# The gate projected and applied token-major in an RWKV-7 mixer layer

## The chip, the cores and the metric
The kernel runs on one core of a Trainium2 chip. The metric is the device time of one execution in microseconds (us). The engines are TensorE (PE), VectorE (DVE), ScalarE (ACT), GpSimd (POOL) and SyncE (SP), which issues most of the transfers.

## The reference
One RWKV-7 time-mixing layer: 2048 tokens, width 1024, 16 heads of 64, all fp32. Cut to what matters:

```python
x_r, x_w, x_k, x_v, x_a, x_g = (h + dx * mu[i] for i in range(6))   # h: normed x
r, k, v = x_r @ W_r, x_k @ W_k, x_v @ W_v
g = silu(x_g @ W_g)
w_lo, a_lo = tanh(x_w @ w_dn), x_a @ a_dn        # low rank: decay and a
def step(S, inp):                                # per head, S is 64 x 64
    sa = einsum('vk,k->v', S, -kk_t)
    S = S * w_t[None, :] + sa[:, None] * (kk_t * a_t)[None, :] + v_t[:, None] * k_t[None, :]
    return S, einsum('vk,k->v', S, r_t)
y = (y - mean) * rsqrt(var + eps)                # per head
y = y * gn_w + gn_b
y = y + sum(r * k * r_k) * v
out = x + (y * g) @ W_out
```

## The kernel before, in words
The tokens are cut into 8 blocks of 256 (`TB`) and 64 chunks of 32 (`L`), the heads into 8 pairs. An fp32 matmul is done as three passes over high and low parts (`passes`, `proj` at L545: high by high, low by high, high by low), 8 column tiles `ct` of the contraction each. The work stands in three stages.

**Stage A** (to about 480 us) loops over the blocks. It norms x into `h`, makes the token-shift mixes of each projection (`mixa` for V, `mixb` for the gate, one buffer each, high and low parts `mixah`, `mixal` and so on), the low-rank products (`lps`, L607), stores the mixes of K and R in DRAM, and then projects. V is token-major: a tile `vps` has 128 tokens by 512 columns, the mix is stationary and 512 columns of W_v move; ACT copies it out (`vo`, L640), DVE subtracts the mean (`vc`, L51), both go to DRAM. The gate is channel-major: a tile `gps` has 128 of W_g's columns by 256 tokens, W_g is stationary and the mix moves, eight tiles a block. `gate` (L195 to L200) applies twice silu: ACT a tanh (`go`), DVE one operation (`go`), and the tile goes to `g_d[b]`, laid out [channel, column tile, token]. The framework's own scheduler orders this stage. In the last block W_r's loads follow.

**Stage B** (to about 1163 us) projects K and R, makes the chunks' operands and inverts their triangular parts; from here on the order is written by hand (`manual_schedule`), each engine in the order in which the program emits. Its end runs the first chunks' recurrence beside the last block.

**The recurrence** (about 1163 to 1656 us). `chunk` issues for each chunk two waves, each of them on PE the state part (`ybank`, L257), the state's update (`dp`, L282), the output part (`ybank`, L293) and `ubank` (L269), with ACT's copies behind them: `misc` L262, `x` L286, `y` L301, `x` L273. Between these, `fill` puts output-projection matmuls (`ops`, L465), by counts `F`. Elementwise work is popped from a queue by `background(BG)`: every step has a price in microseconds and a call spends 1.6 of them; a step of (None, None) ends a call.

The elementwise work is `tail(t)`, t from 0 to 15, one for every four chunks (128 tokens): squares on ACT, variances on DVE, three Newton steps for the reciprocal root on POOL (`rst`, L388), then in four parts of 128x256 the norm (`y<-y,rst` L51, `y<-y,aux` L415) and the bonus (`y<-y,v` L419), all on DVE. Then the two halves k of the tokens are transposed on PE (`yt`, L429, four 128x128 transposes each) into a PSUM bank of a pool `tps` that has one buffer. DVE adds gn_b to it (shift, in PSUM), multiplies it by the gate (gating, `gt<-yt,gt`), ACT takes the high part (`oh`, L444), DVE the low part (`ol`), and 48 output matmuls are queued for `fill`. Their results are added to x (`xr`, L48) and stored. The gate is loaded for the shift's turn from `g_d[b]` in 256-byte pieces, two transfers a tail. Behind the last chunk a loop runs `background(2)` and `fill(6)` until nothing is left.

Of the kernel before, what the change touches and what calls it, by code (L numbers as in the profile page):

```python
# [8 lines left out]
F32 = mybir.dt.float32  # L9
# [9 lines left out]
P = 128  # L19
D = 1024  # L20
# [15 lines left out]
PARAMS = ("norm", "mu_r", "mu_w", "mu_k", "mu_v", "mu_a", "mu_g", "w0", "a0", "k_k", "k_a", "r_k", "gn_b")  # L36
# [3 lines left out]
def rwkv7_kernel(ctx, tc, a, T):  # L40
# [43 lines left out]
    g_d = [dram.tile([P, NCT, TB], F32, name=f"g_d{b}") for b in range(NB)]  # L84
# [4 lines left out]
    # W_out's rows in the place of two blocks' mixes, once those are used  # L89
# [9 lines left out]
    def rsqrt(pool, out, x, shape, nm):  # L99
        # x in SBUF, positive and normal; out may not alias x  # L100
# [23 lines left out]
    def load_w(src, nm, stage, eng=lambda i: None):  # L124
        # steps that load a weight's rows, the row blocks in turn, and the access to its parts
# [24 lines left out]
    def load_wc(src, nm, stage):  # L150
        # the same by column blocks
# [25 lines left out]
    def load_mix(k, mix, b, pool=False, n=NCT // 2):  # L177
        # a projection's mix of the rows, 0: k, 1: r; the steps that split it
# [26 lines left out]
    # of half h: partitions of the K|V and of the B|U parts; columns of the A and of the R part  # L205
# [36 lines left out]
    def decay(ch):  # L242
        # diagonal blocks beside the token-major [K|B]: the chunk's decay of the state
# [59 lines left out]
    def chunk(ch, state, fill):  # L303
        # the recurrence's step, the second wave's end of the chunk before within it
# [28 lines left out]
    def fill(n):  # L333
        # n of the output projection's matmuls between the recurrence's small ones
# [9 lines left out]
    def tail(t):  # L344
        # norm, bonus, gate and output of chunks 4t to 4t + 3, in steps
# [74 lines left out]

        def transpose(k):
# [14 lines left out]
        four = lambda z: z.rearrange("p (h j) t -> p h j t", h=2)  # L436
# [54 lines left out]
    def inversion(g, z, tmp):  # L491
        # z: strict parts, rows (h, chunk, pair); their unit triangular inverses go into M
# [16 lines left out]
    with ExitStack() as p0:  # L509
# [37 lines left out]
        with ExitStack() as pa:  # L547
# [25 lines left out]
            # low rank weights of a token's own and of the token before's normed row  # L573
# [9 lines left out]
            def split_up():  # L583
                # the up projections' weights in high and low parts, stacked to contract at once
                for q in range(2):
                    ups = stage(f"ups{q}")
                    nc.sync.dma_start(ups, a["up"][:, 512 * q : 512 * q + 512])
                    parts = [sp.tile([P, 512], F32R, name=f"up{x}{q}", tag="vo") for x in "hl"]
# [7 lines left out]
            for b in range(NB):  # L596
# [36 lines left out]
                for n in range(2):  # L633
                    for q in range(2):
# [4 lines left out]
                        vo = sp.tile([P, 8, N], F32, name=f"vo{b}{q}{n}", tag="vo")  # L639
# [5 lines left out]
                        vc = sp.tile([P, 8, N], F32, name=f"vc{b}{q}{n}", tag="vo")  # L645
# [8 lines left out]
                for i in range(NCT):  # L654
                    ps = pps.tile([P, TB], F32, name=f"gps{b}{i}", tag="vg")
                    sl = slice(i * P, (i + 1) * P)
                    proj(ps, lambda c: wg[0](c, sl), lambda c: wg[1](c, sl), lambda c: mgh[:, c], lambda c: mgl[:, c])
                    gate(b, i, ps, sp)

        with ExitStack() as pb:  # L660
# [63 lines left out]
            def tokenmajor(c, bank):  # L724
                # [P = (j, i, h; 32), TB] sums to token-major [P, 2, (h, i, j)]
# [47 lines left out]
            def split_lo(b, raw):  # L773
                # high parts twice, beside the low ones: the up projections contract both parts of their weights at once
# [69 lines left out]
            def r_proj(b, p, ps):  # L844
                # the projection's matmuls in two halves
# [466 lines left out]
```

## Time and profile before

| | |
|---|---|
| runs | 1656.64, 1653.35, 1651.27 us |
| median | 1653.35 us |
| profiled execution | span 1656.3 us (of the runs, the one of 1656.64 us is nearest to it), granted clock 0.980 in the mean |
| PE, DVE, ACT, POOL busy | 94%, 71%, 56%, 35% of the span |
| DMA | 269.15 MB, 163 GB/s |

The span runs from the first to the last instruction. A busy PE is modelled, since matmuls overlap: the time that a matmul occupies PE is read from the distance of starts, not from its duration. The number behind x is how many instructions a row holds, and a bracket with an arrow tells how long the engine was idle ahead of the row and what ended that.

### The profile page before, as it was taken

The numbers are of one execution on the slowest core, as the hardware profiler recorded it, in microseconds if no ns is written. First come the engines' busy times: TensorE is split into PE (matmuls) and PEld (weight loads), VectorE is DVE, ScalarE is ACT, GpSimd is POOL, SyncE is SP. The second block draws the span as 40 slices with busy tenths as digits, with TensorE's granted clock in tenths as the row PEclk, the third lists the DMA queues.
The fourth block names the chain that finished last, engine by engine and source line by source line (L and its number), as shares of the span: only waits on it lengthen the run. The fifth ranks groups of instructions, "written<-read, shape, count | busy, mean of one in ns | idle before, by whom it ended". The sixth has DMA issues, their size and how long they took to land.

```text
span 1656.3 us, 46156 instructions
## 1 busy us (share of the span) xinstructions
PE 1549.2 (94%) x17776; PEld 1311.4 (79%) x17776; DVE 1179.6 (71%) x2592; ACT 932.4 (56%) x2378; POOL 573.1 (35%) x911
## 2 busy tenths in 40 slices
PE   3799999999999999989898989899999999999998
PEld 2589889998798887878787878787677777777776
DVE  7976776667656679897988888857646755765454
ACT  5653332233356455445445454588888778877771
POOL 4500000000002334333334343554556555565541
PEclk9899999999999999999999999999999999999999
DMA  5773433334563565656565657787877677667652
GB/s 183 223 259 125 141 124 106 128 125 155 156 215 111 131 136 134 130 152 139 149 151 144 146 145 150 186 223 222 208 202 197 179 189 201 175 167 206 176 126 86
DMA packets 445740, 269.15 MB, mean 163 GB/s; under 512 B 302768, under 2 KB 386096, under 8 KB 445520
## 3 DMA queue, kind: packets, MB, share of 16 engines
q1 hardware_dynamic: 444176, 261.67, 58.9%
q10 hardware_dynamic: 1344, 4.52, 0.9%
q8 instruction: 141, 2.31, 0.6%
q14 instruction: 79, 0.65, 0.1%
HBM read 158.74 MB, written 111.54 MB: 163 GB/s over the span
## 4 chain that ended last, share of the span: by engine, by line
PE 54%; DVE 20%; issue 6%; DMA 6%; ACT 5%; POOL 3%; SPq 0%; DVEq 0%; POOLq 0%; ACTq 0%
PE ops L465 11%; PE gps L545 10%; PE vps L545 5%; PE kps L545 4%; PE ybank L257 4%; PE rps L851 4%; PE ybank L293 3%; DVE th L809 3%; PE dp L282 3%; PE ubank L269 3%; DVE z L51 2%; DVE tm L51 2%; PE mps L887 2%; DVE bk L51 1%; PE lps L607 1%
## 5 line engine op out<-in xcount | busy, mean ns | idle before, releaser
L545 PE MATMUL gps<-mixbh,wgh 128*128 128x256 f32 x512 | 146.9, 287 | 5.0 <-ACT vo L640 5.0
L247 POOL TENSOR_TENSOR dk<-consts,misc 64x512 f32<-64x512 f32 x128 | 144.3, 1127 | 9.3
L545 PE MATMUL gps<-mixbl,wgh 128*128 128x256 f32 x512 | 146.7, 286 | 0.0
L545 PE MATMUL gps<-mixbh,wgl 128*128 128x256 f32 x512 | 146.7, 286 | 0.0
L545 PE MATMUL kps<-mixbl,wkh 128*128 128x256 f32 x448 | 130.7, 292 | 14.8 <-DVE mixbl L186 14.8
L851 PE MATMUL rps<-mixah,wrh 128*128 128x256 f32 x448 | 132.8, 296 | 2.1 <-ACT sq L60 2.1
L545 PE MATMUL kps<-mixbh,wkh 128*128 128x256 f32 x448 | 134.2, 300 | 0.2 <-DVE u L48 0.2
L545 PE MATMUL kps<-mixbh,wkl 128*128 128x256 f32 x448 | 129.8, 290 | 0.0
L851 PE MATMUL rps<-mixal,wrh 128*128 128x256 f32 x448 | 127.2, 284 | 0.0
L851 PE MATMUL rps<-mixah,wrl 128*128 128x256 f32 x448 | 127.1, 284 | 0.0
L60 ACT ACTIVATE th<-wa,dprm 128x256 f32<-128x256 f32 x64 | 30.4, 475 | 169.4 <-PE wa L803 93.9
L841 POOL TENSOR_TENSOR ra<-th,e 128x256 f32<-128x256 f32 x56 | 47.8, 854 | 211.6 <-DVE th L48 207.6
L97 POOL TENSOR_TENSOR upl<-ups,uph 128x512 fp32r<-128x512 f32 x2 | 2.6, 1287 | 336.3 <-DMA up_d<-uph 333.0
L222 POOL MEMSET x<- 32x512 f32 x128 | 66.4, 519 | 145.4 <-PE ybank L293 137.3
L545 PE MATMUL vps<-wvh,mixah 128*128 128x512 f32 x256 | 106.3, 415 | 5.8 <-ACT mixah L96 4.5
L262 ACT COPY misc<-ybank 32x256 f32<-32x256 f32 x220 | 79.9, 363 | 55.7 <-PE ybank L257 52.0
L465 PE MATMUL ops<-woh,oh 128*128 128x512 f32 x256 | 109.5, 428 | 1.6 <-ACT oh L444 1.6
L465 PE MATMUL ops<-woh,ol 128*128 128x512 f32 x256 | 110.4, 431 | 0.0
L465 PE MATMUL ops<-wol,oh 128*128 128x512 f32 x256 | 107.2, 419 | 0.0
L545 PEld LDWEIGHTS gps<-mixbh,wgh 128*128 128x128 f32 x512 | 99.9, 195 | 5.4 <-ACT vo L640 5.4
L545 PE MATMUL vps<-wvl,mixah 128*128 128x512 f32 x256 | 103.5, 404 | 0.0
L545 PEld LDWEIGHTS kps<-mixbl,wkh 128*128 128x128 f32 x448 | 89.1, 199 | 16.0 <-DVE mixbl L186 16.0
(326 smaller groups left out, 4909.4 us busy)
## 6 DMA issues: line engine op xcount, KB each, us to landing
stat<-sm_d SPq DMA_DIRECT2D x64, 512.0 KB, 5.0
dk<-bt_d SPq DMA_DIRECT2D x128, 128.0 KB, 4.6
sm_d<-ra SPq DMA_DIRECT2D x112, 128.0 KB, 3.2
sm_d<-mo SPq DMA_DIRECT2D x112, 128.0 KB, 2.7
bt_d<-bo SPq DMA_DIRECT2D x56, 256.0 KB, 3.3
up<-up_d SPq DMA_DIRECT2D x66, 128.0 KB, 2.7
xn<-x SPq DMA_DIRECT2D x32, 256.0 KB, 4.4
mkr_d<-mok SPq DMA_DIRECT2D x64, 128.0 KB, 1.9
```

The source lines that it names most:

```text
L51: return nc.vector.tensor_tensor(out=out, in0=in0, in1=in1, op=op)
L222: nc.gpsimd.memset(x[bu(h), h], 0.0)
L247: nc.gpsimd.tensor_tensor(out=dk[ch % len(dk)][H, h], in0=ident[H, None, H].broadcast_to([64, NP, N]), in1=pls[g][H, c, :, None].broadcast ...
L257: nc.tensor.matmul(y[half(h), p], st[:, h, 4 * w + p], x[:, h, 4 * w + p], start=(p == 0), stop=(p == 3), tile_position=(0, 64 * h))
L262: nc.scalar.copy(gs[bu(h)], y[kv(h)])
L269: nc.tensor.matmul(bank[2][rb, p], st[rb, h, 4 * w + p, ca], gs[rb, p], start=True, stop=True, tile_position=(rb.start, rb.start))
L282: nc.tensor.matmul(dp[half(1 - h), p], d[:, h, 4 * w + p], x[:, h, 4 * w + p], start=True, stop=True, tile_position=(0, 64 * (1 - h)))
L293: nc.tensor.matmul(bank[w][rb, ch % 2, p], st[rb, h, 4 * w + p, cr], x[rb, h, 4 * w + p], start=False, stop=(p == 3), skip_group_check=Tru ...
L465: nc.tensor.matmul(ps, l[:, ct], r(ct, ns), start=(ct == 0 and k == 0), stop=(ct == NCT - 1 and k == 2))
L545: nc.tensor.matmul(ps, x, y, start=first, stop=last)
L809: nc.vector.tensor_tensor_scan(th, rmask.rearrange("p c l -> p (c l)"), th, 0.0, mul, add)
L851: nc.tensor.matmul(ps, x, y, start=first, stop=last)
```

## The change
The gate's projection takes V's form: 128 tokens by 512 columns, the mix stationary, 512 columns of W_g moving, four tiles a block, and `gate` evacuates tiles of 128x512 (`go` shares the three buffers of `vo` and `vc`). `g_d` becomes one [token, channel] table with rows of 2 KB for a transfer. The tail loads it ahead of the norm, in four transfers, and applies gn_b and the gate to the token-major y in SBUF: a new step `gating(c)` of two DVE operations of 128x256 behind each part's bonus. gn_b moves from the column parameters to `aux`, beside gn_w. Behind the transposes stands only the split: `high` (ACT, `oh` from PSUM) and `rest` (DVE, `ol` from PSUM and `oh`). Shift and the old gating fall away. `rest(0)` is emitted behind the second transposes and their `high`.

```diff
-    def gate(b, i, ps, pool, tag="go", bufs=2):
-        go = pool.tile([P, TB], F32, name=f"go{b}_{i}", tag=tag, bufs=bufs)
+    def gate(rows, ns, ps, pool, nm):
+        go = pool.tile([P, 512], F32, name=f"go{nm}", tag="vo", bufs=3)
         act(go, ps, AF.Tanh, scale=0.5)
         stt(go, go, 1.0, ps, add, mul)
-        nc.sync.dma_start(g_d[b][:, i], go)
+        nc.sync.dma_start(g_d[rows, ns], go)
...
+        def gating(c):
+            x, i = y[part(c)], part(c)[2]
+            tt(x, x, al["gb"][:, i], add)
+            tt(x, x, st["g", c // 2][:, i], mul)
...
         def load_gate(k):
-            st["g", k] = al["gt"](f"gt{t}{k}")
-            nc.sync.dma_start(st["g", k], g_d[b][:, :, q * P + 64 * k : q * P + 64 * k + 64])
+            st["g", k] = g = al["gt"](f"gt{t}{k}")
+            r0 = t * P + 64 * k
+            for h in range(2):
+                nc.sync.dma_start(g[half(h)], g_d[r0 : r0 + 64, 512 * h : 512 * h + 512].rearrange("t (p n) -> t p n", n=N))
...
-        def shift(k):
-            gb = prm[:, PI["gn_b"]].rearrange("p (h j) -> p h j", h=2)
-            tt(turn(k), turn(k), gb[..., None].broadcast_to([P, 2, 4, 64]), add)
-
-        def gating(k):
-            tt(four(st["g", k]), turn(k), four(st["g", k]), mul)
-            nc.scalar.copy(st["oh"][:, :, 64 * k : 64 * k + 64], st["g", k])
+        def high(k):
+            nc.scalar.copy(four(st["oh"], k), turn(k))
 
         def rest(k):
-            tok = slice(64 * k, 64 * k + 64)
-            tt(st["ol"][:, :, tok], st["g", k], st["oh"][:, :, tok].bitcast(F32), sub)
+            tt(four(st["ol"], k), turn(k), four(st["oh"], k).bitcast(F32), sub)
...
+        out.append((0.0, lambda: (load_gate(0), load_gate(1))))
         for c in range(4):
             out.append((0.7, lambda c=c: norm(c)))
             out.append((0.4, lambda c=c: bonus(c)))
+            out.append((0.7, lambda c=c: gating(c)))
         cut = len(out)
-        out.append((0.0, lambda: (load_gate(0), load_gate(1))))
         for k in range(2):
-            out.extend([(None, None), (0, lambda k=k: transpose(k)), (None, None)])
+            out.extend([(None, None), (0, lambda k=k: transpose(k)), (None, None), (0, lambda k=k: high(k))])
             if k == 1:
                 out.append((0.7, lambda: rest(0)))
-            out.append((0.7, lambda k=k: shift(k)))
-            out.append((0.7, lambda k=k: gating(k)))
         out.append((0.7, lambda: rest(1)))
...
-                for i in range(NCT):
-                    ps = pps.tile([P, TB], F32, name=f"gps{b}{i}", tag="vg")
-                    sl = slice(i * P, (i + 1) * P)
-                    proj(ps, lambda c: wg[0](c, sl), lambda c: wg[1](c, sl), lambda c: mgh[:, c], lambda c: mgl[:, c])
-                    gate(b, i, ps, sp)
+                for n in range(2):
+                    for q in range(2):
+                        rows, ns = slice((2 * b + q) * P, (2 * b + q + 1) * P), slice(n * 512, (n + 1) * 512)
+                        ps = pps.tile([P, 512], F32, name=f"gps{b}{q}{n}", tag="vg")
+                        proj(ps, lambda c: mgh[:, c, q * P : (q + 1) * P], lambda c: mgl[:, c, q * P : (q + 1) * P],
+                             lambda c: wg[0](c, ns), lambda c: wg[1](c, ns))
+                        gate(rows, ns, ps, sp, f"{b}{q}{n}")
```

How the change moves instructions shows at three places. In the rows yt120 is the bank's tile of tail 12, half 0, and yt121 that of half 1; y12 is the tail's normed y, ops110 an output tile of tail 11; the numbers behind an underscore are buffers.

First PE's queue between the two transposes of tail 12, in the changed kernel:

```order
L434 MATMUL yt120_21093<-consts_60,y12_19756 128x128 x4
L282 MATMUL dp_14785<-x1_12923,dk2_12920 64x64 x8
L466 MATMUL ops110_21072<-wol1_13498,oh11_20641 128x512
L466 MATMUL ops110_21072<-woh1_13497,ol11_20642 128x512
L293 MATMUL ybank1_14783<-x1_12923,stat2_12916 32x64 x8
L269 MATMUL ubank_14784<-misc_12911,stat3_12917 32x64 x8
L466 MATMUL ops110_21072<-woh2_13689,oh11_20641 128x512
L466 MATMUL ops110_21072<-wol2_13690,oh11_20641 128x512
L466 MATMUL ops110_21072<-woh2_13689,ol11_20642 128x512
L466 MATMUL ops110_21072<-woh3_13870,oh11_20641 128x512
L257 MATMUL ybank1_14783<-x2_12924,stat3_12917 64x64 x8
L434 MATMUL yt121_21154<-consts_60,y12_19756 128x128 x4
```

One wave, with six output matmuls, stands between the two sets, as it did before; what the second set waits for has changed from DVE's gating to DVE's `ol` of the first half.

Second ACT's queue at the same place: before (first fence) and in the changed kernel (second).

```order
L273 COPY x1_13858<-ubank_15713 32x256 x2
L262 COPY misc_13846<-ybank1_15712 32x256 x2
L444 CAST oh12_21613<-gt120_21562 128x8x64
L286 COPY x2_13859<-dp_15714 64x256 x2
L301 COPY y13_21264<-ybank0_15711 32x256 x2
```

```order
L301 COPY y14_20799<-ybank1_14783 32x256 x2
L273 COPY x2_12924<-ubank_14784 32x256 x2
L446 CAST oh12_21091<-yt120_21093 128x8x64
L262 COPY misc_12911<-ybank1_14783 32x256 x2
L286 COPY x0_12922<-dp_14785 64x256 x2
```

The cast of the first half's high part stood behind `misc` and read SBUF; now it stands between the wave's last copy `x` and the next wave's `misc`, and reads the bank.

Third DVE's queue at the same tail: before (first fence) and in the changed kernel (second).

```order
L419 TENSOR_TENSOR y12_20740<-y12_20740,v12_1_21301 128x256
L48 SCALAR_TENSOR_TENSOR xr1010_21427<-ops101_21426,xr1010_21427 128x256
L48 SCALAR_TENSOR_TENSOR xr1011_21429<-ops101_21426,xr1011_21429 128x256
L51 TENSOR_TENSOR yt120_21615<-yt120_21615,prm_62 128x2x4x64
L51 TENSOR_TENSOR gt120_21562<-yt120_21615,gt120_21562 128x512
L51 TENSOR_TENSOR ol12_21614<-gt120_21562,oh12_21613 128x8x64
L51 TENSOR_TENSOR yt121_21678<-yt121_21678,prm_62 128x2x4x64
L51 TENSOR_TENSOR gt121_21564<-yt121_21678,gt121_21564 128x512
L51 TENSOR_TENSOR ol12_21614<-gt121_21564,oh12_21613 128x8x64
```

```order
L51 TENSOR_TENSOR y12_19756<-y12_19756,rst12_20744 128x256
L415 TENSOR_TENSOR y12_19756<-y12_19756,aux_12912 128x256
L419 TENSOR_TENSOR y12_19756<-y12_19756,v12_1_20748 128x256
L48 SCALAR_TENSOR_TENSOR xr1010_20836<-ops101_20835,xr1010_20836 128x256
L48 SCALAR_TENSOR_TENSOR xr1011_20838<-ops101_20835,xr1011_20838 128x256
L51 TENSOR_TENSOR y12_19756<-y12_19756,aux_12912 128x256
L51 TENSOR_TENSOR y12_19756<-y12_19756,gt121_20898 128x256
L51 TENSOR_TENSOR ol12_21092<-yt120_21093,oh12_21091 128x8x64
L51 TENSOR_TENSOR ol12_21092<-yt121_21154,oh12_21091 128x8x64
```

Each part of y has five operations instead of three, and the two `ol` now stand together behind all twenty, with nothing between them.

## Rows read from the trace of the kernel before

**Rows 1.** The page: busy time, share of the span and instructions of each engine

```profile
PE 1549.2 (94%) x17776; PEld 1311.4 (79%) x17776; DVE 1179.6 (71%) x2592; ACT 932.4 (56%) x2378; POOL 573.1 (35%) x911
```

**Rows 2.** Stretches: us; busy (x) PE, PEld, DVE, ACT, POOL; PEclk, DMA share, GB/s

```profile
240.00:280.00 40.00, 40.00 (x280) 37.51 (x280) 25.45 (x67) 10.78 (x27) 0.00 (x0) 1.00 0.36 123
...
1400.00:1500.00 100.00, 99.35 (x1763) 74.75 (x1763) 70.66 (x142) 80.50 (x218) 57.93 (x96) 1.00 0.68 180
```

**Rows 3.** The chain of waits in stage A: start us, us, what

```profile
145.93 17.27 PE gps L545 x144
...
163.79 8.20 PE vps L545 x36
```

**Rows 4.** PE's timeline in the recurrence: start us, us, instruction, count

```profile
1388.22 0.69 PE L257 MATMUL ybank<-x,stat 128*64 128x64 f32 x16
...
1391.64 0.69 PE L257 MATMUL ybank<-x,stat 128*64 128x64 f32 x16
1392.25 0.66 PE L429 MATMUL yt<-consts,y 128*128 128x128 f32 x4
...
1395.79 0.69 PE L257 MATMUL ybank<-x,stat 128*64 128x64 f32 x16
```

**Rows 5.** ACT's timeline: the same waves, and a cast near the end

```profile
1391.30 0.76 ACT L273 COPY x<-ubank 32x256 f32<-32x256 f32 x2
1392.42 0.75 ACT L262 COPY misc<-ybank 32x256 f32<-32x256 f32 x2 [0.37 <-PE ybank L257]
...
1620.56 0.62 ACT L444 CAST oh<-gt 128x512 fp32r<-128x512 f32 x1
```

**Rows 6.** Stage A's evacuations by form: duration in ns, min/median/max

```profile
L48 DVE SCALAR_TENSOR_TENSOR go<-go,gps x64: 409/421/423, 88.2 to 480.2; 128x256 f32<-128x256 f32 x64
...
L640 ACT COPY vo<-vps x32: 574/587/590, 73.4 to 463.1; 128x512 f32<-128x512 f32 x32
...
L51 DVE TENSOR_TENSOR vc<-vo,mn x32: 677/691/694, 77.8 to 466.9; 128x512 f32<-128x512 f32 x32
```

**Rows 7.** The chain of waits at the end of stage A

```profile
479.74 0.39 ACT go L60
...
480.16 0.43 DVE go L48
```

**Rows 8.** DVE in the recurrence, by line and form: busy us, mean ns

```profile
L51 DVE TENSOR_TENSOR yt<-yt,prm 128x512 f32<-128x512 f32 x32 | 22.2, 694 | 7.2 <-PE yt L429 7.1
...
L415 DVE TENSOR_TENSOR y<-y,aux 128x256 f32<-128x256 f32 x61 | 41.9, 687 | 2.1
```

**Rows 9.** PE's timeline at tail 5's second transposes

```profile
1322.78 0.69 PE L257 MATMUL ybank<-x,stat 128*64 128x64 f32 x16
...
1325.89 0.63 PE L429 MATMUL yt<-consts,y 128*128 128x128 f32 x4 [0.52 <-DVE gt L51]
...
1327.97 0.69 PE L257 MATMUL ybank<-x,stat 128*64 128x64 f32 x16 [0.74 <-ACT y L301]
```

**Rows 10.** The end: PE's timeline and DVE's

```profile
1619.11 0.64 PE L293 MATMUL ybank<-x,stat 32*32 32x64 f32 x16
...
1633.22 0.44 PE L429 MATMUL yt<-consts,y 128*128 128x128 f32 x2 [1.26 <-DVE y L419]
...
1637.23 0.63 PE L429 MATMUL yt<-consts,y 128*128 128x128 f32 x4 [0.58 <-DVE gt L51]
...
1621.82 0.41 DVE L384 TENSOR_REDUCE var<-sq 128x4 f32<-128x256 f32 x1
...
1628.29 1.25 DVE L51 TENSOR_TENSOR y<-y,rst 128x256 f32<-128x256 f32 x1 [4.00 <-POOL rst L388]
```

**Rows 11.** DVE and POOL in the recurrence: y beside a scaling of v

```profile
1383.50 1.25 DVE L51 TENSOR_TENSOR y<-y,rst 128x256 f32<-128x256 f32 x1 [2.55 <-POOL rst L388]
...
1386.36 0.42 DVE L51 TENSOR_TENSOR y<-y,rst 128x256 f32<-128x256 f32 x1
...
1383.42 2.23 POOL L367 TENSOR_TENSOR v<-v,misc 128x512 f32<-128x512 f32 x2
```

More of the change, by code (lines that the diff above doesn't have):

```diff
@@ L35 @@
 GN_EPS = 64e-5
-PARAMS = ("norm", "mu_r", "mu_w", "mu_k", "mu_v", "mu_a", "mu_g", "w0", "a0", "k_k", "k_a", "r_k", "gn_b")
+PARAMS = ("norm", "mu_r", "mu_w", "mu_k", "mu_v", "mu_a", "mu_g", "w0", "a0", "k_k", "k_a", "r_k")
 PI = {n: i for i, n in enumerate(PARAMS)}
@@ L83, in rwkv7_kernel @@
     vc_d = dram.tile([T, D], F32, name="vc_d")
-    g_d = [dram.tile([P, NCT, TB], F32, name=f"g_d{b}") for b in range(NB)]
+    g_d = dram.tile([T, D], F32, name="g_d")
     lo_d = [dram.tile([P, TB], F32, name=f"lo_d{b}") for b in range(NB)]
@@ L431, in load_gate @@
         def load_gate(k):
-            st["g", k] = al["gt"](f"gt{t}{k}")
-            nc.sync.dma_start(st["g", k], g_d[b][:, :, q * P + 64 * k : q * P + 64 * k + 64])
+            st["g", k] = g = al["gt"](f"gt{t}{k}")
+            r0 = t * P + 64 * k
+            for h in range(2):
+                nc.sync.dma_start(g[half(h)], g_d[r0 : r0 + 64, 512 * h : 512 * h + 512].rearrange("t (p n) -> t p n", n=N))
         turn = lambda k: st["ps", k].rearrange("p j (h t) -> p h j t", h=2)
-        four = lambda z: z.rearrange("p (h j) t -> p h j t", h=2)
-        def shift(k):
-            gb = prm[:, PI["gn_b"]].rearrange("p (h j) -> p h j", h=2)
-            tt(turn(k), turn(k), gb[..., None].broadcast_to([P, 2, 4, 64]), add)
-        def gating(k):
-            tt(four(st["g", k]), turn(k), four(st["g", k]), mul)
-            nc.scalar.copy(st["oh"][:, :, 64 * k : 64 * k + 64], st["g", k])
+        four = lambda z, k: z[:, :, 64 * k : 64 * k + 64].rearrange("p (h j) t -> p h j t", h=2)
+        def high(k):
+            nc.scalar.copy(four(st["oh"], k), turn(k))
         def rest(k):
-            tok = slice(64 * k, 64 * k + 64)
-            tt(st["ol"][:, :, tok], st["g", k], st["oh"][:, :, tok].bitcast(F32), sub)
+            tt(four(st["ol"], k), turn(k), four(st["oh"], k).bitcast(F32), sub)
         def load_x(n, q):
@@ L587, in split_up @@
                     nc.sync.dma_start(ups, a["up"][:, 512 * q : 512 * q + 512])
-                    parts = [sp.tile([P, 512], F32R, name=f"up{x}{q}", tag="vo") for x in "hl"]
+                    parts = [sp.tile([P, 512], F32R, name=f"up{x}{q}", tag="vo", bufs=3) for x in "hl"]
                     split(*parts, ups, nc.gpsimd)
@@ L638, in rwkv7_kernel @@
                              lambda c: wv[0](c, ns), lambda c: wv[1](c, ns))
-                        vo = sp.tile([P, 8, N], F32, name=f"vo{b}{q}{n}", tag="vo")
+                        vo = sp.tile([P, 8, N], F32, name=f"vo{b}{q}{n}", tag="vo", bufs=3)
                         nc.scalar.copy(vo, ps.rearrange("p (h n) -> p h n", n=N))
@@ L644, in rwkv7_kernel @@
                         ts(mn, mn, 1.0 / N, None, mul)
-                        vc = sp.tile([P, 8, N], F32, name=f"vc{b}{q}{n}", tag="vo")
+                        vc = sp.tile([P, 8, N], F32, name=f"vc{b}{q}{n}", tag="vo", bufs=3)
                         tt(vc, vo, mn[:, :, None].broadcast_to([P, 8, N]), sub)
@@ L900, in preload @@
                 al["gw"] = aux[:, 0:512].rearrange("p (h n) -> p h n", n=N)
-                al["aux"] = iter(aux[:, x : x + 16].rearrange("p (k h) -> p k h", k=2) for x in range(512, 1024, 16))
-                nc.sync.dma_start(al["gw"], a["gn_w"].rearrange("p (h n) -> p h n", n=N))
+                al["gb"] = aux[:, 512:1024].rearrange("p (h n) -> p h n", n=N)
+                al["aux"] = iter(misc[0][:, x : x + 16].rearrange("p (k h) -> p k h", k=2) for x in range(736, 1024, 16))
+                nc.sync.dma_start(aux, a["gn_wb"])
                 stat.extend(wtile(f"stat{i}", [P, 2, NP, 64], F32) for i in range(4))
@@ L1148, in rwkv7_kernel @@
                 al["yt"] = lambda nm: aps_.tile([P, 4, P], F32, name=nm, tag="wa0")
-                al["gt"] = lambda nm: kp.tile([P, NCT, 64], F32, name=nm, tag="rk", bufs=4)
+                al["gt"] = lambda nm: kp.tile([P, NP, N], F32, name=nm, tag="rk", bufs=4)
                 early = deque()
@@ L1196, in rwkv7_kernel @@
         al["yt"] = lambda nm: tps.tile([P, 4, P], F32, name=nm, tag="tps")
-        al["gt"] = lambda nm: yp.tile([P, NCT, 64], F32, name=nm, tag="gt", bufs=2)
+        al["gt"] = lambda nm: yp.tile([P, NP, N], F32, name=nm, tag="gt", bufs=2)
         def background(us):
@@ L1293, in layout @@
         "up": c(np.concatenate([f("l0_w_up"), f("l0_a_up")], axis=0)[:, perm]),
-        "gn_w": c(np.repeat(f("l0_gn_w").reshape(2, 8 * N), 64, axis=0)), "w_out": c(f("l0_w_out")),
+        "gn_wb": c(np.repeat(np.concatenate([f(n).reshape(2, 8 * N) for n in ("l0_gn_w", "l0_gn_b")], axis=1), 64, axis=0)),
+        "w_out": c(f("l0_w_out")),
     }
```

2 lines of the change are left out of this document (1 added, 1 removed).

## The prediction

> **What bounds the kernel now.** I read the page first: in one execution TensorE (PE) is at work in nearly every slice [rows 1]. The share is an average over stages, so I read it by stage, in the table by stretch: in the gate's and V's projections 40.00 of 40 us, and in the recurrence 99.35 of 100, while VectorE (DVE) has 70.66 and ScalarE (ACT) 80.50 of 100 there [rows 2]. In both stages a microsecond is won only by issuing fewer or shorter matmuls, and lost by anything that makes PE wait. The granted clock is 1.00, the upper level of 2.4 GHz, in both, so I price no step by the clock.
>
> The chain of waits gives the spacing: 144 gate matmuls of 256 columns in 17.27 us are 0.120 us each, 36 V matmuls of 512 columns in 8.20 us are 0.228 us each [rows 3].
>
> In the recurrence PE's timeline shows the pattern: a wave begins with the 16 ybank of L257 and holds four or more output matmuls. One with four takes 3.42 us (1388.22 to 1391.64), the next, with four and the four transposes yt, 4.15 us [rows 4]. PE's queue is full from end to end. ACT has room for 0.37 to 0.7 us between its copies of two waves [rows 5].
>
> **The change, part by part.** *Gate projection.* Per block 192 matmuls of 256 columns become 96 of 512 columns: 192 x 0.120 = 23.0 us against 96 x 0.228 = 21.9 us, a gain of 1.17 us, 9.4 us for eight blocks. The row bears the wider form, since V's projection is built in the same way from the same kind of tiles. What feeds the stage could take some of it back (DVE makes the next block's mixes, 25.45 of 40 us there [rows 2]) or add to it: four DVE evacuations of 0.69 us, the price of vc, its nearest operation of 128x512, replace eight of 0.42 us [rows 6], so DVE has about 0.6 us per block more for mixes. I take 11 us, with ends 8 and 15.
>
> The Trainium skill, page "TensorE: Matmul & The Clock Gate", section "Back-to-back issue gap", gives one matmul a gap of its columns over 2.4 GHz plus 2.5 ns. By that the 768 matmuls saved are worth only 768 x 2.5 ns = 1.9 us, and the sum below would be 9 us higher. The trace does not bear it out: two narrow ones cost 0.240 us here, one wide one 0.228.
>
> At the end of the stage nothing covers the last evacuation: ACT go, DVE go [rows 7], then the issue of its store and the load of W_r behind it on SP's queue. ACT's tile goes from 0.39 us to the 0.59 us of vo, DVE's from 0.43 to 0.69 us [rows 6]: **+0.5 us**.
>
> *The gate's traffic.* Stores are 32 of 256 KB in 2-KB rows instead of 64 of 128 KB, loads 2048-byte packets instead of 256-byte ones, but four issues a tail instead of two, on SP's queue. Loads are now issued ahead of the norm, and no row of PE before waits for them: 0, with ends -1 and +1.
>
> *The tail's DVE work.* The shift and gating, four operations of 128x512 at 0.69 us that read PSUM, become eight of 128x256 on SBUF. The same kind (y with aux) costs 0.687 us in the mean there [rows 8], so 5.5 us against 2.8 per tail. DVE has 30 of 100 us free [rows 2], which covers 2.7 us per tail of some 30 us; what that costs where it is not covered is in the two next steps.
>
> *The PSUM bank.* There is one bank for yt. Before, it came free when DVE's gating had read it; now both ACT's cast oh and DVE's subtraction ol read it, so the second set of transposes, yt(1), waits for oh(0) and then ol(0). The order shows where ACT's oh(0) stands for tails 1, 4 to 8 and 11 to 13: behind the last copy x of the wave, while on PE only 16 ybank stand between that wave and yt(1). Worked out on the waves in rows 4 and 5: the copy x ends at 1392.06, oh takes 0.62 [rows 5], ol 0.69 like the shift, which reads the bank in the same form [rows 8], hops some 0.15, so yt(1) could begin at 1393.5 where PE reaches it at 1392.25: **1.1 to 1.2 us lost in each of 9 tails, 10 us**. That nothing absorbs such a stall shows in tail 5 before, the one place in the recurrence where PE came to yt(1) too early: it waited 0.52 us for DVE and the wave behind another 0.74 us for ACT, and the wave took 5.19 us instead of about 4.15 [rows 9]. Tail 9's two sets are consecutive on PE, and there ol(0) comes behind the twenty y operations: 2 to 5 us; tail 10 some 0.6 us. Tails 2 and 3 have two waves between and cost nothing. Together **+13 us**, with ends 6 (half of the stalls hidden) and 20 (ol(0) late behind a y operation in every tail).
>
> *The end.* By the order 42 more output matmuls and eight more transposes stand behind the last L293 than before (171 and 16, against 129 and 8): tail 14's norm has moved past it. The matmuls are moved, not added: 42 x 0.228 = 9.6 us less before it, as much behind it. What is added is idle time. Before, the 129 matmuls from 1619.11 hid most of tail 15's norm, whose first y came 9.2 us later, at 1628.29, behind 4.00 us of POOL's Newton steps; PE lost only 1.26 and 0.58 us before the two sets [rows 10]. Now the sequence happens twice. For tail 14, counted from the last L293: var and g take some 2.5 us (before from 1621.82 to 1624.29, where the wait of 4.00 begins [rows 10]), Newton 4.0, so the first y stands at +6.5; ten y operations of 0.69 us last to +13.4, and PE, with 48 output matmuls of 0.228 us ahead, is at yt(0) at +10.9 and waits for the last two of its transposes some 2.1 us. The other ten, which POOL disturbs less, at 0.53 us last to +18.7 and ol(0) to +19.4; PE, 12 matmuls on, is there at +16.5: 3 us. For tail 15 its squares stand behind oh(14) on ACT, the same Newton steps follow and then again twenty operations instead of twelve: by the same count 2.4 us before yt(0) and 3.9 us before yt(1), where only 59 and 8 output matmuls stand ahead. That is 11 us idle against about 2: **+9 us**, with ends 5 and 12.
>
> *Between.* Tail 0, in the flush ahead of the recurrence, has consecutive sets too, but other work of PE's is due there: +0.5, ends 0 and 1.
>
> The sum: -11 + 0.5 + 0 + 13 + 9 + 0.5 = **+12 us**. It is made against the profiled execution (1656.3 us span), which stands 0.2% above the median of the runs, 1653.35. On that median it gives **1665 us**. Its own ends: -15 + 0.5 - 1 + 6 + 5 = -4.5, and -8 + 0.5 + 1 + 20 + 12 + 1 = +26.5; all ends at once are unlikely, so I take 1653 to 1676 as this case's own.
>
> **The rivals.** *A, the gain is kept (faster).* The mechanism is PE's gate spacing with its waits hidden: if oh(0) runs in ACT's gap before the wave's x copy is due and ol(0) is on DVE at once, yt(1) meets a free bank. It decides if the stalls in the nine tails come below 0.5 us, 4 us in all, and the end adds 3 us: -13 + 0.5 + 4 + 3, some 5 us under the median, **1647 us**. For it speaks that DVE and ACT have 30 and 20 of 100 us free [rows 2]; against it, ACT's place in the order and tail 5 [rows 9].
>
> *B, it cancels.* The stalls are half as dear and the end likewise: -11 + 1 + 6 + 4, **1653 us**.
>
> *C, DVE becomes late everywhere (worse).* A y operation took 1.25 us while POOL scaled v, and 0.42 us behind it [rows 11]. If all eight new ones meet POOL at 1.2 us they cost 9.6 us a tail instead of the 5.5 taken; ol(0), behind them on DVE, is then a further 1 us late in some ten tails, and the end's two tails idle 2 us more each: +12 + 10 + 4, **1679 us**. The share of POOL at work, 57.93 of 100 us, says that about half of them meet it, which the mean has in it [rows 2]. The Trainium skill, "SBUF — State Buffer", sections "SBUF: two separate sides" and "Who interferes with whom", says that DVE with two SBUF inputs and a GpSimd operation that reads SBUF take an exclusive lock, the later one blocked; the pair of rows agrees in kind.
>
> *D, the wide gate doesn't pay.* If stage A goes at the pace of DVE's mixes, the -11 shrinks to 0 and the rest stays: +23, **1676 us**. Against it: PE has 40.00 of 40 us there [rows 2].
>
> **How the numbers follow.** Forecast 0.52 (its own range 1653 to 1676), A 0.18, B 0.14, C 0.10, D 0.06. Faster or slower means by over 0.3%, 5 us, about what a measurement of this kernel can tell: below 1648.4 lies most of A and a little of B's spread, 0.18; between, B's rest and the low end of the forecast, 0.20; above 1658.3 the rest, 0.62. The range that leaves 2 in 10 out takes half of A in and most of C: 1646 to 1678.
>
> **What would show it.** Right: gps of 512 columns at 0.228 us and a block's period in stage A about 1.3 us shorter, so that stage B begins some 10 us sooner; PE yt in the recurrence with a wait of about 1 us on DVE ol in most tails; more than 40 us between the last L293 and the end. Wrong: yt(1) without idle time ahead of it (A), gps spacing above 0.235 us or idle time ahead of vps that is not there before (D), y operations that average over 0.9 us (C), or stage B not beginning earlier.

## The result and the profile after

The changed kernel takes 1662.62 us in the median (1658.19 to 1664.95), the kernel before 1653.91: slower by 0.55%, ratio 1.0055 with a 95% interval of 1.0036 to 1.0074. The forecast was 1665 us, slower. The profiled execution of the changed kernel has a span of 1661.7 us. I read it by stage, first the spacing and the end of stage A.

The chain of waits in stage A of the changed kernel (start us, us, what):

```profile
147.10 16.35 PE gps L545 x72
...
462.22 0.61 ACT go L60
...
462.85 0.70 DVE go L48
```

72 wide matmuls take 16.35 us, 0.227 us each, where 144 narrow ones took 17.27 [rows 3]. The last evacuation lasts what the prediction gave it (0.61 and 0.70 us), but it ends at 463.55 us, where it ended at 480.59 before [rows 7]: the stage is 17.0 us shorter, not the 10.5 of the forecast.

PE's side of the transposes yt in the changed kernel (idle time of PE ahead of them by releaser: us, times):

```profile
its engine sat idle before it (us, times) until:
  DVE ol L51: 17.9, 10
  DVE y L51: 0.8, 2
```

Before, PE lost 2.4 us ahead of yt in the whole program; now it waits ten times for `ol`. PE's timeline shows eight of these twelve waits (start us, us, instruction, idle ahead):

```profile
1326.18 0.63 PE L434 MATMUL yt<-consts,y 128*128 128x128 f32 x4 [1.34 <-DVE ol L51]
...
1437.08 0.63 PE L434 MATMUL yt<-consts,y 128*128 128x128 f32 x4 [1.34 <-DVE ol L51]
1474.23 1.12 PE L434 MATMUL yt<-consts,y 128*128 128x128 f32 x4 [4.09 <-DVE ol L51]
...
1538.30 0.66 PE L434 MATMUL yt<-consts,y 128*128 128x128 f32 x4 [0.76 <-DVE ol L51]
...
1617.95 0.44 PE L434 MATMUL yt<-consts,y 128*128 128x128 f32 x2 [0.32 <-DVE y L51]
1623.72 1.09 PE L434 MATMUL yt<-consts,y 128*128 128x128 f32 x4 [2.56 <-DVE ol L51]
...
1637.96 0.44 PE L434 MATMUL yt<-consts,y 128*128 128x128 f32 x2 [0.51 <-DVE y L51]
1643.52 0.66 PE L434 MATMUL yt<-consts,y 128*128 128x128 f32 x4 [3.27 <-DVE ol L51]
```

In the recurrence seven of them add up to 10.2 us: tails 5, 6 and 8 (1.34, 1.09, 1.34), tail 9 whose two sets are consecutive (4.09), tails 10 to 12 (0.82, 0.76, 0.80). Behind the last L293 the four come to 6.7 us, against 1.26 + 0.58 before [rows 10]. One more, of 1.81 us, lies in tail 0.

How one arises stands in ACT's, DVE's and PE's timelines at tail 8:

```profile
1435.63 0.58 ACT L446 CAST oh<-yt 128x512 fp32r<-128x512 f32 x1
...
1436.25 0.69 DVE L51 TENSOR_TENSOR ol<-yt,oh 128x512 fp32r<-128x512 f32 x1 [3.29 <-ACT oh L446]
...
1435.06 0.69 PE L257 MATMUL ybank<-x,stat 128*64 128x64 f32 x16
1437.08 0.63 PE L434 MATMUL yt<-consts,y 128*128 128x128 f32 x4 [1.34 <-DVE ol L51]
```

PE is through the 16 ybank at 1435.75. ACT has only just begun to cast the first half out of the bank, `ol` follows at once, and only when that ends at 1436.94 is the bank free. DVE sat idle for 3.29 us ahead of `ol`: what was late is the cast, by its place in ACT's queue.

The table sets the four stretches side by side; a stretch runs from the first L257 on `ybank` to the last L293 (starts), and the end from there to the end of the span.

| us | before | changed | difference |
|---|---|---|---|
| end of the gate's last evacuation | 480.59 | 463.55 | -17.0 |
| first L257 of the recurrence | 1170.0 | 1154.3 | -15.7 |
| recurrence, L257 to last L293 | 449.5 | 451.8 | +2.3, with 42 output matmuls and 8 transposes fewer in it |
| last L293 to the end | 36.8 | 55.6 | +18.8, with 42 output matmuls and 8 transposes more |

All 768 output matmuls stand behind the first L257 in both kernels, so what the recurrence gave up the end received: 42 matmuls of 0.228 us and eight transposes of some 0.165 us, 10.9 us in all. The recurrence so lost 13.2 us and the end 7.9 us. Of the 17.0 us won, 1.3 were lost again ahead of the recurrence. Together that is the difference of the two profiled executions, +5.4 us.

### The profile page after: what moved, and what is told of

Read it like the earlier page. It is cut to its first block, busy times and chain, and to the rows that moved or that the text cites. A ratio compares the mean times of both kernels' runs of the same rounds, so it can differ in the third digit from the quotient of the medians.

```text
span 1661.7 us, 44585 instructions
## 1 busy us (share of the span) xinstructions
PE 1537.7 (93%) x17008; PEld 1269.9 (76%) x17008; DVE 1207.9 (73%) x2624; ACT 925.1 (56%) x2346; POOL 564.4 (34%) x911
## 4 chain that ended last, share of the span: by engine, by line
PE 56%; DVE 19%; ACT 6%; issue 5%; DMA 5%; POOL 3%; SPq 1%; DVEq 0%; POOLq 0%; ACTq 0%
PE ops L466 10%; PE gps L545 9%; PE vps L545 8%; PE kps L545 5%; PE ybank L257 4%; DVE th L811 3%; PE rps L853 3%; PE ybank L293 3%; PE dp L282 3%; PE ubank L269 2%; DVE z L51 2%; DVE tm L51 2%; PE lps L607 2%; DVE bk L51 2%; PE mps L889 2%
## 5 line engine op out<-in xcount | busy, mean ns | idle before, releaser
L247 POOL TENSOR_TENSOR dk<-consts,misc 64x512 f32<-64x512 f32 x128 | 138.0, 1078 | 9.3
L545 PE MATMUL gps<-wgh,mixbh 128*128 128x512 f32 x256 | 99.9, 390 | 1.5 <-DVE go L48 1.5
L545 PE MATMUL gps<-wgl,mixbh 128*128 128x512 f32 x256 | 99.8, 390 | 0.0
L545 PE MATMUL gps<-wgh,mixbl 128*128 128x512 f32 x256 | 99.7, 390 | 0.0
L257 PEld LDWEIGHTS ybank<-x,stat 128*64 128x64 f32 x1760 | 62.1, 140 | 43.8 <-issue 16.9
```

The source lines that it names most:

```text
L247: nc.gpsimd.tensor_tensor(out=dk[ch % len(dk)][H, h], in0=ident[H, None, H].broadcast_to([64, NP, N]), in1=pls[g][H, c, :, None].broadcast ...
L257: nc.tensor.matmul(y[half(h), p], st[:, h, 4 * w + p], x[:, h, 4 * w + p], start=(p == 0), stop=(p == 3), tile_position=(0, 64 * h))
L545: nc.tensor.matmul(ps, x, y, start=first, stop=last)
```

## The experiments

Each was timed beside the kernel before on the same chip. The first two take the change apart.

**The projection alone.**

```diff
-    def gate(b, i, ps, pool, tag="go", bufs=2):
...
+    def gate(dst, ps, pool, nm):
...
-                for i in range(NCT):
...
+                for n in range(2):
+                    for q in range(2):
...
+                        gate(g_d[b][:, i : i + 2].rearrange("p c t -> p (c t)"), ps, sp, f"{b}{q}{n}")
```

> The kernel before with the new gate projection alone (96 matmuls of 512 columns a block, tiles of 128x512), its tail unchanged. The tiles go into the old table without regard to its layout, so the gate that the tail applies is wrong, its traffic on the load side is the old one. My theory: the stage ends some 17 us earlier as in the changed kernel (463.55 against 480.59) and nothing gives it back but the 1 to 2 us seen at stage B's end (15 to 16 us at the recurrence's first state matmul): 1638 us, 1635 to 1642, against 1654 before. Rival: only the matmuls' spacing pays (9.4 us) and the rest of the 17 us came with the new tail's traffic: 1645. Rival: a later stage waits for something else and takes the gain back: 1650 or more.

Measured: 1641.01 us against 1655.28, ratio 0.9916 (0.9893 to 0.9939), 14 us faster, inside the range. The projection is a gain of its own, and it doesn't need the new tail. In its profile the first L257 of the recurrence stands 19 us earlier than before (1150.8 against 1170.0), and 4 of these are given back in the recurrence, whose length is 453.6 us against 449.5: in its first 40 us the granted clock is 0.87 in the mean, against 0.96 before. The first 40 us of the recurrence in the kernel before, then with the projection alone (start:end, us; busy time and count of PE, PEld, DVE, ACT, POOL; granted clock, DMA share, GB/s):

```profile
1170.00:1210.00 40.00, 37.92 (x660) 28.09 (x661) 20.22 (x39) 32.48 (x88) 22.67 (x40) 0.96 0.76 189
```

```profile
1150.80:1190.80 40.00, 37.58 (x598) 28.08 (x598) 19.08 (x35) 29.21 (x79) 18.94 (x33) 0.87 0.82 206
```

What brings the clock down there wasn't tried. The tail has no part in it here, since it is the old one.

**The tail alone.** The changed kernel with the old projection:

```diff
-        nc.sync.dma_start(g_d[rows, ns], go)
+        nc.sync.dma_start(g_d[b * TB + 32 * i : b * TB + 32 * i + 32].rearrange("t (k n) -> (t k) n", n=TB), go)
...
-                for n in range(2):
-                    for q in range(2):
...
+                for i in range(NCT):
...
```

> The changed kernel with the old gate projection (192 matmuls of 256 columns a block); its tiles go into the new table without regard to its layout, so the gate is wrong. The tail is the new one. My theory: the tail costs 13 us in the recurrence and 8 behind the last L293, 24 with the 2 to 3 us lost ahead of it: 1677 us, 1673 to 1682. Rival: the tail is nearly free and the changed kernel lost its stage A gain in another way: below 1665.

Measured: 1677.49 us, ratio 1.0134 (1.0119 to 1.0149), 22 us slower. Recurrence and end have the lengths of the changed kernel (451.8 and 55.6 us) to the tenth, and yt waits 17.5 us for `ol`. So the change is a gain of 14 and a loss of 22 us that add up: their sum, +8, is the change's +8.7 within its interval.

**Two banks.** The next three ask whether the one bank is the cause. The first attempt made room by putting two small tiles of the recurrence into one bank:

```diff
-        bank[2] = sps.tile([P, 4, N], F32, name="ubank")
-        bank[3] = sps.tile([P, 4, N], F32, name="dp")
+        ud = sps.tile([P, 2, 4, N], F32, name="ubdp")
+        bank[2], bank[3] = ud[:, 0], ud[:, 1]
...
-        al["yt"] = lambda nm: tps.tile([P, 4, P], F32, name=nm, tag="tps")
+        al["yt"] = lambda nm: tps.tile([P, 4, P], F32, name=nm, tag="tps", bufs=2)
```

> The changed kernel with two PSUM banks for the transposes (two small recurrence tiles share one bank to make room); PE's order is the same. My theory: the one bank makes yt(1) wait for ol(0). With two, the waits of 10.2 us in the recurrence go, the slow-clock stretch behind the one of 4.09 us (some 2.5 us) too, and of the 5.8 us behind the last L293 half: 1662.6 - 10 - 2.5 - 3 = 1647, 1643 to 1652. Rival: the second transposes are late because the twenty y operations are, and they wait for y in place of ol: 1657 to 1663.

Measured: 1681.71 us, ratio 1.0166 (1.0149 to 1.0183): slower, against both theories. One of its PE groups in the recurrence says why (busy us, mean ns, idle ahead and its releaser):

```profile
L269 PE MATMUL ubdp<-misc,stat 32*32 32x64 f32 x1760 | 70.4, 218 | 21.4 <-ACT x L286 21.4
```

The shared tile made the `ubank` matmuls wait for ACT's copy of `dp`, 21.4 us that the changed kernel doesn't have. The `yt` waits for `ol` fell to one of 1.4 us even here, but the run's time is that of its own edit. It was made again with the bank taken from the output tiles, beside a control:

```diff
-                st[n] = sps.tile([P, 512], F32, name=f"ops{t}{n}", tag="dense", bufs=3)
+                st[n] = sps.tile([P, 512], F32, name=f"ops{t}{n}", tag="dense", bufs=2)
...
-        al["yt"] = lambda nm: tps.tile([P, 4, P], F32, name=nm, tag="tps")
+        al["yt"] = lambda nm: tps.tile([P, 4, P], F32, name=nm, tag="tps", bufs=2)
```

> The changed kernel with two banks for the transposes, the second taken from the output tiles (two instead of three); every small recurrence tile keeps its own bank. PE's order is the same as in the changed kernel. My theory: the waits of yt(1) for ol(0) go (10.2 us in the recurrence, half of the 5.8 us behind it, 1.8 in tail 0), and the slow-clock stretches behind the long ones with them, some 4 us: 1662.6 - 10 - 3 - 4 = 1646, 1642 to 1653, if its control with two output tiles and one bank stays within 3 us of the changed kernel. Rival: yt(1) then waits for y instead: 1657 or more.

> Control: the changed kernel with two output tiles in place of three and one bank for the transposes. My theory: the evacuations keep up, so 1660 to 1666. Rival: the third output tile matters: 1667 or more, and the two-bank run has to be read against this one.

Measured: the control, with the first edit alone, 1664.74 us, ratio 1.0052 (1.0033 to 1.0071), as the changed kernel; with both edits 1649.75 us, ratio 0.9968 (0.9950 to 0.9985). The second bank is worth 15 us: it is the one bank that cost the greater part of the tail's 22. The change with it is 0.3% faster than the kernel before. PE's side of yt in the control, then with two banks:

```profile
its engine sat idle before it (us, times) until:
  DVE ol L51: 17.9, 10
  DVE y L51: 0.9, 2
```

```profile
its engine sat idle before it (us, times) until:
  DVE y L51: 7.5, 7
  DVE ol L51: 1.4, 1
```

The waits for `ol` are gone but for one in tail 0, which still takes its bank from stage B's pool. The recurrence lasts 442.5 us in place of the control's 452.1, the end 51.2 in place of 55.6. What is left are waits for y: 2.4 us in tail 9 and 5.1 us in the end's two tails. The clock of the recurrence's first 40 us, 0.90 in the mean, has not come back: it isn't the bank's doing.

**The end.** The next runs try to bring tail 14 back ahead of the last L293.

```diff
-            out.append((0.7, lambda c=c: gating(c)))
+            out.append((0.2, lambda c=c: gating(c)))
...
-            out.extend([(None, None), (0, lambda k=k: transpose(k)), (None, None), (0, lambda k=k: high(k))])
-            if k == 1:
-                out.append((0.7, lambda: rest(0)))
-        out.append((0.7, lambda: rest(1)))
+            out.extend([(None, None), (0, lambda k=k: transpose(k)), (None, None), (0, lambda k=k: high(k)),
+                        (0.7, lambda k=k: rest(k))])
```

> The changed kernel with one bank, the gating step priced 0.2 instead of 0.7 in the queue of elementwise steps and ol(0) emitted ahead of the second transposes, so that tail 14 is normed and transposed ahead of the last L293 again (123 output matmuls behind it instead of 171) and a wave with four to six output matmuls stands between the two sets in every tail. My theory: the waits behind the last L293 fall from 6.7 us to some 2 us, and the waits for the bank become some 0.8 to 1.3 us in up to 14 tails, 13 us in all against 10: 1662.6 - 5 - 2 + 3 = 1658, 1652 to 1662. Rival: the price is only bookkeeping, DVE falls behind and the waits get longer: 1665 or more.

Measured: 1693.52 us, ratio 1.0232 (1.0212 to 1.0251): the rival's side, and further. With one bank, PE's side of yt:

```profile
its engine sat idle before it (us, times) until:
  DVE ol L51: 27.5, 16
  DVE y L51: 7.0, 6
```

My theory fell here. A step's price is more than bookkeeping: it holds PE's transposes back until DVE is through, and at 0.2 they stand where DVE is still at y, in nearly every tail. Of the 16 `ol` that PE waited for, 14 started on DVE right behind a y operation. The clock is part of the loss: its mean over the recurrence is 0.957, against 0.983 in the changed kernel. The edit has two parts, the price and the place of `ol(0)`, which weren't taken apart.

**A shorter hold, and POOL adds gn_b.** ACT empties the bank, gn_b goes into v:

```diff
+            nc.gpsimd.tensor_tensor(out=st["v", k], in0=st["v", k], in1=al["gb"], op=add)
...
-            tt(x, x, al["gb"][:, i], add)
...
+            nc.scalar.copy(chan(k), turn(k))
...
-            nc.scalar.copy(four(st["oh"], k), turn(k))
+            nc.scalar.copy(four(st["oh"], k), chan(k))
...
-            out.append((0.7, lambda c=c: gating(c)))
+            out.append((0.4, lambda c=c: gating(c)))
...
```

> The changed kernel with three edits meant to win its loss back: ACT empties the bank into the freed gate tile in one copy, and both parts are taken from there; gn_b is added to the scaled v by POOL, so that DVE has four operations of y in a part instead of five; the gating step is priced 0.4, so that tail 14 stands ahead of the last L293 (132 output matmuls behind it). My theory: what holds the bank is then one copy of 0.62 us, the wait of yt(1) falls to 0.5 us in each of 13 tails, and the end has one tail again (8 us less): 1662.6 - 6 - 8 - 4 = 1645, 1640 to 1651. Rival: DVE or POOL fall behind, as DVE did with the cheap price alone, and yt waits for y: 1665 or more.

Measured: 1670.14 us, ratio 1.0075 (1.0050 to 1.0101). The hold itself is cured, six waits for ACT's copy add up to 2.7 us; but yt waits 14.2 us for y. The rival held; which of the three edits makes y late, this run can't tell. To keep POOL's part and drop the rest, the same edit of gn_b was made on the two-bank kernel, with a lower price:

```diff
+            nc.gpsimd.tensor_tensor(out=st["v", k], in0=st["v", k], in1=al["gb"], op=add)
...
-            tt(x, x, al["gb"][:, i], add)
...
-            out.append((0.7, lambda c=c: gating(c)))
+            out.append((0.35, lambda c=c: gating(c)))
```

> The changed kernel with two banks (two output tiles), gn_b added to the scaled v by POOL (two operations of 128x512 a tail), so that DVE has sixteen operations of y in place of twenty, each step of gating priced 0.35, which moves all tails forward (122 output matmuls behind the last L293). My theory: DVE's work is then as dear against its price as before the change, so it keeps up: 1649.8 - 3 - 2 - 1 = 1644, 1639 to 1650. Rival: POOL hands v over 2.2 us later and disturbs DVE longer, and y comes late as with the short hold: 14 us of waits for y, 1655 or more.

Measured: 1669.59 us, ratio 1.0084 (1.0056 to 1.0111); yt waits 18.4 us for y. Here DVE's groups decide: first the two-bank kernel, then this one (busy us, mean ns, idle ahead).

```profile
L51 DVE TENSOR_TENSOR y<-y,rst 128x256 f32<-128x256 f32 x60 | 48.8, 813 | 53.0 <-POOL rst L388 53.0
L415 DVE TENSOR_TENSOR y<-y,aux 128x256 f32<-128x256 f32 x60 | 41.6, 693 | 2.1
L51 DVE TENSOR_TENSOR y<-y,gt 128x256 f32<-128x256 f32 x60 | 39.6, 660 | 2.1
L419 DVE TENSOR_TENSOR y<-y,v 128x256 f32<-128x256 f32 x60 | 30.3, 506 | 3.8
L51 DVE TENSOR_TENSOR y<-y,aux 128x256 f32<-128x256 f32 x60 | 29.7, 495 | 1.9
```

```profile
L51 DVE TENSOR_TENSOR y<-y,gt 128x256 f32<-128x256 f32 x60 | 56.1, 935 | 2.4 <-DMA gt<-g_d 0.4
L51 DVE TENSOR_TENSOR y<-y,rst 128x256 f32<-128x256 f32 x60 | 52.6, 876 | 64.7 <-POOL rst L389 64.7
L416 DVE TENSOR_TENSOR y<-y,aux 128x256 f32<-128x256 f32 x60 | 41.4, 689 | 2.1
L420 DVE TENSOR_TENSOR y<-y,v 128x256 f32<-128x256 f32 x60 | 37.0, 617 | 3.1
```

Sixty operations are gone, and DVE's time for y has hardly changed: 190.0 us with twenty a tail, 187.1 us with sixteen. What they cost, the others now pay beside POOL's longer work: y<-y,gt rose from 660 to 935 ns. The lower price isn't what lengthens them: in the cheap-step run, over all sixteen tails, DVE spends 199.9 us on y, as in the two-bank kernel. As the work is as long as before and its price lower, PE comes too early, as with the cheap step. POOL's addition at the old price of 0.7 wasn't run, so what it costs by itself stays open.

**Cheap only where DVE has room.** On the two-bank kernel, the gating step priced 0 from tail 11 on, and `ol(0)` ahead of the second transposes:

```diff
-            out.append((0.7, lambda c=c: gating(c)))
+            out.append((0.0 if t >= 11 else 0.7, lambda c=c: gating(c)))
...
```

> The changed kernel with two banks (two output tiles), ol(0) ahead of the second transposes, and the gating step priced 0 from tail 11 on alone, where the inversion's work on DVE is done: tail 14 stands ahead of the last L293 again (131 output matmuls behind it instead of 171). My theory: against the two-bank kernel (1649.8) the end idles for one tail only and tail 9's wait goes: 3 and 2 us less, 1645, 1641 to 1649. Rival: DVE is behind in tails 11 to 14 too, as it was in all with the cheap price, and PE waits for y there: 1650 or more.

Measured: 1651.11 us, ratio 0.9966 (0.9949 to 0.9982), the same as two banks alone. The end is down from 51.2 to 37.8 us, the recurrence up from 442.5 to 457.7. The work moved back, some 10.4 us (40 matmuls and 8 transposes), so the end won 3.0 us and the recurrence lost 4.8: tail 9 still waits (3.5 us in three parts) and tail 11 now waits 1.96 us. Neither theory is borne out whole: the time is the rival's, but of tails 11 to 14 only tail 11 waits.

**A narrow token-major gate.** What of the stage's 17 us is width?

```diff
-                for i in range(NCT):
...
+                for n in range(4):
+                    for q in range(2):
+                        i, ns = 2 * n + q, slice(n * TB, (n + 1) * TB)
...
```

> The kernel before with the gate token-major but only 256 columns moving (192 matmuls of 256 columns a block, tiles of 128x256, the mix stationary); its tiles go into the old table without regard to its layout, so the gate is wrong. It has the token-major order without the wider matmul. My theory: the spacing stays 0.120 us, so the 9.4 us don't come and only what the order and the mix's release give remains: 0 to 5 us under the kernel before. Rival: the order of release is what pays, not the width: 10 us or more under it. Rival: nothing remains, or it is slower, since with narrow tiles the weight loads repeat: within 3 us or above.

Measured: 1656.59 us, ratio 1.0004 (0.9986 to 1.0021). Token-major order alone is worth nothing; the last rival held, and all of the gain comes with the width. With it comes more than the spacing. The narrow run keeps not only the 0.120 us but also a wait of PE in the last block's gate, which the kernel before has and the wide ones don't (first before, then narrow):

```profile
456.78 0.58 PE L545 MATMUL gps<-mixbh,wgh 128*128 128x256 f32 x1 [3.13 <-ACT vo L640]
```

```profile
456.13 0.58 PE L545 MATMUL gps<-wgh,mixbh 128*128 128x256 f32 x1 [2.78 <-ACT vo L640]
```

## Why the prediction was right

**Direction and size.** 1665 us was forecast, 1662.62 measured, slower as forecast. That it came so close is partly luck. The sum of +12 was made against the profiled execution; between the two profiled executions it came out as +5.4: -17.0 for stage A, where -10.5 was forecast, +1.3 between (+0.5), +13.2 in the recurrence (+13) and +7.9 at the end (+9). The medians differ by 8.7, since single executions of one kernel differ by some us. Stage A is the term that was mis-sized, and in the two terms that fit, parts that were too large stand against a clock that wasn't priced.

**The gate projection was mis-sized**: -11 was taken, with ends 8 and 15; the stage gave 17.0 us, and the projection alone 14 in the whole. The spacing was right: 0.227 us against the 0.228 taken, 9.8 us for eight blocks. What was missed is idle time of PE, because the stretch that the prediction read, 240 to 280 us [rows 2], happens to hold none. From the second block's gate to the last block's PE idled 3.2 us before the change, nearly all of it for ACT's casts of a mix (`mixah`) and copies of a V tile (`vo`), and 0.2 us after.

The last block cost more. There PE waited 3.13 us (the row shown with the narrow gate) until ACT had copied out the V tile whose bank the second gate tile needs, and then the granted clock was at its lower level:

```profile
456.80:462.00 5.20, 5.20 (x24) 5.20 (x25) 4.31 (x11) 2.56 (x7) 0.00 (x0) 0.50 1.03 383
```

That block's gate matmuls took 28.9 us where 192 x 0.120 is 23.0; the difference is the wait and some 2.8 us of the slow clock. The changed kernel's took 21.8 us, without a wait. Part of the reason can be read from the rows: a narrow tile keeps PE busy for 2.9 us before it needs the next bank, a wide one for 5.4 us. The other part is that ACT's copy ended 6.1 us after the block's first gate matmul before and 2.9 us after it now; why it comes earlier wasn't tried apart. The prediction had this place in view ("what feeds the stage"), but weighed DVE there, and PE waited for ACT.

Spacing, waits and clock make 18.7 us; another 1.7 lie at V's matmuls and the statistics' `bcpa`, unexplained, and 0.5 go to the longer evacuation. That this execution shows 17.0 and not 19.9 is due to the time ahead of the second block's gate, where executions differ; the projection alone shows 19.0.

The Trainium skill's rule that was weighed ("TensorE: Matmul & The Clock Gate", "Back-to-back issue gap"), which that page calls the gap of an isolated matmul, made the saving 1.9 us; the spacing in the trace makes it 9.8, five times as much.

**The bank**: +13 was forecast, 13.2 measured. The mechanism is the one named, as the second bank shows; that the size fits is luck. Of the nine tails expected to lose 1.1 to 1.2 us, 10 us in all, five did, 0.76 to 1.34 us, 5.3 in all; tails 1, 4, 7 and 13 didn't, because I took their order to be that of tail 12: in them the cast stands behind `misc`, and a `ubank` comes ahead of yt(1) on PE, which so arrives when the bank is free. Tail 9 cost 4.09 us, within 2 to 5. The yt waits are 10.2 us. What made up for the missing stalls is the clock, which the prediction left out with the words "I price no step by the clock": some 2.6 us behind tail 9's wait (PE's timeline from 1474.2 to 1480.2), and in the recurrence's first 40 us a granted clock of 0.89 against 0.96, which is up to 2.5 us more. The latter isn't the bank's: the projection alone has it too, and so has the kernel with two banks.

**The end**: +9 was forecast, 7.9 measured, again in other parts. The waits before yt(0) were 0.3 and 0.5 us, not 2.1 and 2.4. For tail 14 the first y stood at +6.0, not +6.5, ten operations lasted 6.6 us, not 6.9 (only the first two met POOL), and PE, whose matmuls ahead I had counted from the start of the last L293 and not from its end, was there at +12.0, not +10.9. Those before yt(1) were 2.56 and 3.27, as expected (3.0 and 3.9). The four are 4.8 us more than the two of before; the other 3 us are about what the two stretches at half clock behind them cost (below).

**The rivals.** A (the gain kept) asked for stalls below 0.5 us in the nine tails; four met that, five didn't, and the end added 7.9 us, not 3. The second bank frees yt(1) in another way than A's; that its 1649.8 lies near A's 1647 is chance. B's halved stalls came true for the nine tails, but not for the rest. C, DVE late everywhere, isn't the changed kernel, whose y operations take 0.63 us in the mean, but the one with the cheap step and those with POOL's additions. D fell with the projection alone.

## What to carry to other kernels

Before an elementwise step is moved across a transpose, ask what will hold the PSUM bank afterwards: here two engines in a row in place of one, with the first queued behind the recurrence's copies, cost 15 us, as much as the projection won. A change with a gain in one stage and a loss in another is best run in halves: the whole said +9, the halves -14 and +22, and most of the loss had a cure in one more bank. A stage in which PE looks full should be read to its last block before it is priced by the spacing alone. Where an order is made from prices, the price of a step is also the distance that keeps a consumer on another engine from coming too early.

## What was not expected of the hardware

**The clock can fall behind a long wait, and then the wait is paid twice.** Stretches of the changed kernel behind the three longest waits for `ol` (start:end, us; busy time and count of PE, PEld, DVE, ACT, POOL; granted clock, DMA share, GB/s):

```profile
1474.00:1478.00 4.00, 3.77 (x24) 2.70 (x24) 0.39 (x2) 2.04 (x5) 0.00 (x0) 0.50 0.62 197
1624.00:1627.00 3.00, 3.00 (x10) 2.52 (x9) 1.54 (x4) 1.82 (x5) 0.00 (x0) 0.50 0.68 193
1644.00:1647.00 3.00, 3.00 (x10) 2.36 (x9) 1.35 (x3) 0.59 (x1) 0.00 (x0) 0.51 0.19 55
```

PE had waited 4.09, 2.56 and 3.27 us; the granted clock was then 0.50, the lower level of 1.2 GHz. PE's timeline behind the first of them shows the price (start us, us):

```profile
1476.87 0.63 PE L466 MATMUL ops<-woh,oh 128*128 128x512 f32 x1
1477.30 0.63 PE L466 MATMUL ops<-wol,oh 128*128 128x512 f32 x1
1477.72 0.63 PE L466 MATMUL ops<-woh,ol 128*128 128x512 f32 x1
```

The output matmuls start 0.425 us apart, not 0.228. Behind the waits of 0.8 to 1.3 us nothing of the kind stands in the stretches of 40 us (clock 1.00). But not every longer wait does it either. In stage B of the same trace PE waits 2.57 us for DVE in block after block; behind some of these the clock is 0.50, behind this one it stays at 1.00:

```profile
726.57 0.38 PE L545 MATMUL kps<-mixbl,wkh 128*128 128x256 f32 x1 [2.57 <-DVE mixbl L186]
```

```profile
726.60:730.00 3.40, 3.40 (x29) 3.37 (x29) 2.82 (x9) 1.78 (x6) 0.75 (x2) 1.00 0.51 185
```

In the run with the tail alone, the last block's wait in stage A was 2.67 us and the clock behind it 1.00, where the 3.13 us of before and the 2.78 us of the narrow run were followed by 0.50. What decides was not found.

**Taking work off DVE by giving it to POOL took nothing off DVE.** Two more POOL operations a tail and four fewer on DVE left DVE's time for y at 187 of 190 us. The Trainium skill's page "SBUF — State Buffer", section "Who interferes with whom", says that a DVE operation with two SBUF inputs contends with a GpSimd operation that reads SBUF, and this run agrees in kind. In every tail of the changed kernel there are y operations of about 0.42 us and of 1.1 to 1.3 us [rows 11], and each of the longer ones ran beside an arithmetic operation of POOL's; the 54 that ran beside nothing of POOL's but a memset, which only writes, took 0.39 to 0.43 us.
